# A hybrid encoder layer on one core: attention rotated by one head, three preparations moved

## The chip, the cores and the metric

The kernel runs on one core of one Trainium2 chip. The metric is the device time of one execution in microseconds (us); the median of three runs of the kernel before is 1181.16 us (1180.96 to 1181.49). A difference below 0.2%, about 2.4 us, is counted as no change.

## What is computed

One layer works on 512 prompt tokens and 64 sample tokens (576 columns here) of width 1024. The normed input `h` goes through one wide projection `w_in`, whose columns feed three branches, and the branches are merged by gates:

```python
glu_v, glu_g, conv_gate, z, xbc, dt_raw, q, xa_gate, gates = split(rmsnorm(x) @ w_in)
# A: causal depthwise conv of width 31, LayerNorm over channels
c = dwconv31(glu_v * sigmoid(glu_g))
out_a = (silu(layernorm(c)) * silu(conv_gate)) @ conv_out_w
# B: state-space scan (SSD) in chunks, 4 groups of 8 heads
out_b = (group_norm(ssd(silu(dwconv4(xbc)), dt) * silu(z))) @ ssd_out_w
# C: cross-attention, 4 heads of 256, 256 memory tokens
k, v = rmsnorm(mem) @ xa_kv_w          # the sample uses cached k, v
o = softmax(q k^T / 16) v
out_c = (o * silu(xa_gate)) @ xa_out_w
m = g0 * out_a + g1 * out_b + g2 * out_c
x_new = x + rmsnorm(m @ w_out)
```

Memory keys and values, convolution tails and SSD states are outputs too.

## The kernel before, in words

**Numbers.** Every large product is made in a reduced-width float type from a high and a low part of both operands: each weight `w` becomes `whi` (a copy rounded to that type) and `wlo = w - whi`, and so do the activations. One product is three matmuls: `whi` with the high activations, `whi` with the low, `wlo` with the high (`mac`, L206 to L216, and `proj`, L218). A projection of 128 columns over 576 tokens is 8 x 3 x 2 = 48 matmuls; in the attention a key block is 24 and the values of a head are 48.

**Weights.** The list `order` (L95 to L162) is a hand-written order of weight jobs. `W(name)` (L201) takes one and has `prep_to` prepare jobs up to two further on (LA = 2). Preparing is a load on the SP queue into one of three `raw` buffers, a copy to `whi` on ScalarE (L186), and the low part. Jobs ahead of `hold` (L144) take the low part on VectorE with one subtraction (L188). Jobs from `hold` on write minus `whi` by ScalarE (L190; here the copy of `raw` with scale -1) and add `raw` to it by an accumulating DMA on the POOL queue (L191). `whi` and `wlo` have three buffers each, so the job n+3 waits until the matmuls of job n have read theirs.

**Order of the work.** The program is written in straight line, and the tile framework orders each engine's instructions at build time by priority, which is the order of the program, and by when its own model of the chip thinks that operands and buffers are there. On the chip each engine then runs its list in order.

1. Input norm and transposes; then four SSD groups of five chunks (`chunk_a`, `chunk_b`), with projections (`fills`) as filling between the chunks.
2. Three `glu` tiles (L751; two projections each), in between the group norm of the last SSD group (`gating_b(3)`), then its output projection `out_b(3, 0..3)` (L755). Then the pools of this stage are closed.
3. The **pair phase** (L803 to L992): seventeen pairs of projections made with seven products each instead of eight (Strassen's scheme, products P1 to P7, 12 matmuls each, 119 slots in `seq`). It first builds four combinations of the activations, `T1` to `T4` (`comb`, L810 to L835), in a pool that opens here. `pair_load` fetches weights, `pair_pure` (L858) prepares a weight used alone with the accumulating DMA, `pair_sum` (L867) sums of weights on VectorE. The list `todo` (L973) says how many slots ahead each is issued. Results are attention gates `xg` and the gates `g2`, spilled to memory through the SP queue, the gates `g1`, and five more `glu` tiles.
4. **Attention** (L998 to L1174): memory tokens are loaded, normed (`rms_tile`) and transposed into `memT`; the queries of head 0 are projected ahead. Then, in a loop over four heads: keys and queries, keys to token order and cached keys transposed, values, scores and softmax in three tiles, transposes of the probabilities (L1152), their high and low parts (`pth`, `ptl`), output products, gating into `oc`.
5. `oc` is split into high and low parts, eight output projections `oc0..7` are merged; then LayerNorm sums over the convolution (`ln_mean`, `ln_rstd`), eight `cg` projections (the gate of branch A), eight `g0` projections, the LayerNorm applied tile by tile (L1253 on), eight `oa` projections, then `w_out` and the final norm.

**The convolution of width 31** is 240 instructions on VectorE (L773: 30 taps for each of 8 tiles). They lie in a list `bg`, from which `bgrun(n)` takes the next n and issues them with raised priority: one at every second slot of the pair phase, 44 per head, ten per merge, and all that are left before `ln_mean` (L1243). LayerNorm needs all of them.

**Names in the profile.** `mm<-hT,whi` is a projection of tokens, `ps<-memT,wlo` a key block, `ps<-wlo,memT` a values block; X, Y and Z (L892) are the PSUM tiles of the pair phase; `ct` its result tiles, `raw`/`rawb`, `ph`/`pl` its weights; `mt` the memory tokens; `P` the probabilities; `c` a convolution tile.

Of the kernel before, what the change touches and what calls it, by code (L numbers as in the profile page):

```python
# [8 lines left out]
F32 = mybir.dt.float32  # L9
# [19 lines left out]
def hybrid_trunk_kernel(  # L29
# [110 lines left out]
    for j in range(3):  # L140
        glu_jobs(j)
    for q in range(4):
        ob_job(3, q)
    hold = len(order)  # L144
    for h in range(4):
        if h == 0:
            for i in range(2):
                wjob(f"q{i}", w_in, C_Q + 128 * i)
        for i in (2 * h, 2 * h + 1):
            wjob(f"k{i}", xa_kv_w, 128 * i)  # L150
            if h > 0:
                wjob(f"q{i}", w_in, C_Q + 128 * i)
        for i in range(2):
            wjob(f"v{h}_{i}", xa_kv_w, 1024 + 256 * h, r0=512 * i, kk=4, cols=256)
# [14 lines left out]
    def prep_to(n):  # L169
        while nprep[0] <= min(n, len(order) - 1, limit[0]):  # L170
# [14 lines left out]
            else:  # L185
                a = nc.scalar.activation(hi[:, :n_], raw[:, :n_], AF.Copy)  # L186
                if nprep[0] < hold:
# [49 lines left out]
    hl = [st.enter_context(tc.tile_pool(name="hl4", bufs=4, reuse_waits="tile"))]  # L237

# [12 lines left out]
    for t in range(5):  # L251
# [3 lines left out]
        else:  # L255
            x_t = s2.tile([128, D], F32, tag="M", name="x4")
        nc.sync.dma_start(out=x_t[:n], in_=xp_d[128 * t:128 * t + 128] if t < 4 else xs_d)
        xt.append((x_t, n))
        if t == 0:
            wpre = s2.tile([128, D], F32, tag="R", name="wpre")  # L260
# [12 lines left out]
    sqx = s2.tile([128, D], F32, tag="M", name="sqx")  # L273
# [62 lines left out]
    eal = s2.tile([128, 32], F32, tag="yo", name="eal", bufs=1)  # L336
    nc.sync.dma_start(out=eal, in_=ssd_a_log[0].partition_broadcast(128))
    after = s2.tile([128, 128], F32, tag="bt", name="after")
# [8 lines left out]
    def dt_proj():  # L347
# [9 lines left out]
        dtv["raw"] = raw = s2.tile([64, 640], F32, tag="M", name="dtraw")  # L357
# [32 lines left out]
    def dt_cum():  # L390
# [13 lines left out]
        acsT = s2.tile([32, 640], F32, tag="M", name="acsT")  # L404
# [5 lines left out]
    vraw = s2.tile([104, 128], F32, tag="cbm", name="vraw")  # L410
# [9 lines left out]
    def load_t(dst, c0, src_ap, n, scale=1.0):  # L420
        raw = s2.tile([128, 128], F32, tag="bt", name="praw")
# [65 lines left out]
    def out_state(h, g, dst):  # L487
# [3 lines left out]
        o = s2.tile([128, 512], F32, tag="hio", name="ho", bufs=1)  # L491
# [8 lines left out]
    def chunk_a(g, c):  # L500
        nl = 128 if c < 4 else 64
        cs = slice(128 * c, 128 * c + nl)
        Rt = s2.tile([128, 8, 128], F32, tag="R", name="R")
# [3 lines left out]
        if c == 4:  # L507
            hin = s2.tile([128, 4, 128], F32, tag="hio", name="hin", bufs=1)
# [18 lines left out]
        cbm = s2.tile([128, 128], F32, tag="cbm", name="cbm")  # L527
        nc.vector.tensor_tensor(cbm[:nl, 0:nl], pc[:nl, 0:nl], mask[:nl, 0:nl], ALU.mult)
        bt = s2.tile([128, 128], F32, tag="bt", name="bt")
# [5 lines left out]
        xw = s2.tile([128, 512], F32, tag="xw", name="xw")  # L535
# [4 lines left out]
        xd = s2.tile([128, 512], F32, tag="xd", name="xd")  # L540
# [4 lines left out]
        cd = s2.tile([128, 8], F32, tag="cd", name="cd")  # L545
        nc.scalar.activation(cd, R[:, :, nl - 1], AF.Exp)
        Mt = s2.tile([128, 8, 128], F32, tag="M", name="M")
# [14 lines left out]
    def chunk_b(g, c, tup):  # L562
# [6 lines left out]
        if h is not None:  # L569
# [233 lines left out]
    def hb(i, j):  # L803
        ks, ts = slice(4 * i, 4 * i + 4), slice(288 * j, 288 * j + 288)
        return hT[0][:, ks, ts], hT[1][:, ks, ts]

# [3 lines left out]
    comb = {k: tuple(sp.tile([128, 4, 288], F32R, name=f"{k}{a}", bufs=1) for a in "hl") for k in ("T1", "T2", "T3", "T4")}  # L810
    for kp in range(2):
        ks = slice(2 * kp, 2 * kp + 2)

        def blk(i, j):
            f = th_tile().rearrange("p (k t) -> p k t", k=2)
            h, l = hb(i, j)
            nc.vector.tensor_tensor(f, h[:, ks].bitcast(F32), l[:, ks].bitcast(F32), ALU.add)
            return f

        def put(name, f):  # L820
            h, l = comb[name]
            nc.scalar.activation(h[:, ks], f, AF.Copy)
            nc.vector.tensor_tensor(l[:, ks], f, h[:, ks].bitcast(F32), ALU.subtract)

        a, b = blk(0, 1), blk(0, 0)
        nc.vector.tensor_tensor(b, b, a, ALU.subtract)
        put("T1", b)
        c = blk(1, 1)
        nc.vector.tensor_tensor(a, c, a, ALU.subtract)
        put("T3", a)  # L830
        nc.vector.scalar_tensor_tensor(c, b, -1.0, c, ALU.mult, ALU.subtract)
        put("T2", c)
        d = blk(1, 0)
        nc.vector.scalar_tensor_tensor(d, c, -1.0, d, ALU.mult, ALU.subtract)
        put("T4", d)  # L835
# [84 lines left out]
    def pair_use(kind, j, c):  # L920
# [11 lines left out]
        else:  # L932
            nc.sync.dma_start(out=spill["g2"][j], in_=c)
# [40 lines left out]
    for p in range(np_):  # L974
# [7 lines left out]
            (at[p, "P4"] - 6, lambda p=p: pair_pure(p, "W22", "P4")),  # L982
# [17 lines left out]
    st = ExitStack()  # L1000
    st3 = ExitStack()
    a2 = st3.enter_context(tc.tile_pool(name="a2", bufs=2, reuse_waits="tile"))
    memp = st3.enter_context(tc.tile_pool(name="memp", bufs=1, reuse_waits="tile"))
    st4 = ExitStack()
    m0 = st4.enter_context(tc.tile_pool(name="m0", bufs=1, reuse_waits="tile"))
    memT = [memp.tile([128, KD, NMEM], F32R, name=f"memT{i}") for i in range(2)]
    mt_ = []
# [398 lines left out]
```

## Time and profile before

| what | before |
|---|---|
| median of 3 runs | 1181.16 us |
| profiled execution, its own time | 1180.58 us |
| span of the profiled instructions | 1178.5 us |
| mean granted TensorE clock | 0.973 |
| TensorE matmul busy | 1113.5 us, 94% |
| VectorE busy | 854.8 us, 73% |
| ScalarE busy | 620.0 us, 53% |
| pair phase (first P2 to last product) | 501.4 to about 719 us |
| attention (first query projection to the first `oc` projection at full rate) | 719.2 to 914.5 us |

How to read it: "busy" is the share of the span in which an engine executes; the granted clock is the share of its full rate that TensorE was allowed. In a row of waits, `PE x Ln <- DMA y: a, b, c` says that instructions of TensorE at line n stood idle for a us in all, b times, at most c us, until a DMA into y had landed. In a row of windows stand the length, each engine's busy time with its number of instructions, the granted clock, the DMA engines' busy share and GB/s. In a group's row the first number behind the bar is the busy time in us, the second the mean of one instruction in ns.

### The profile page before, as it was taken

How to read it: one execution, taken by the hardware profiler on the slowest of the kernel's cores; microseconds unless marked ns; L12 is line 12 of the kernel's file. 1: busy time of each engine (PE TensorE's matmuls, PEld its weight loads, DVE VectorE, ACT ScalarE, POOL GpSimd, SP SyncE). 2: the span in 40 equal slices, each digit the busy share in tenths (PEclk: the TensorE clock that was granted, in tenths of full speed). 3: DMA queues.
4: the chain of work that ended last, by engine and by line, in shares of the span. 5: the costliest groups of instructions: out<-in, count | busy, mean ns of one | idle time of the engine just before them, and what ended most of it. 6: DMA issues, size and time to landing. Idle time of an engine off the chain costs nothing.

```text
span 1178.5 us, 20510 instructions
## 1 busy us (share of the span) xinstructions
PE 1113.5 (94%) x8081; PEld 1061.3 (90%) x8081; DVE 854.8 (73%) x1355; ACT 620.0 (53%) x1081; POOL 157.6 (13%) x253
## 2 busy tenths in 40 slices
PE   8999999999999999969999997788997999999997
PEld 8999999999999999959999997687886999999975
DVE  5878888597879766498888871477878988683433
ACT  5565655383456324266666664656446324684332
POOL 0100200020002001122233211101101111111000
PEclk9999999999999999979999999789988999999999
DMA  7354423432352322475888888669858886778822
GB/s 198 92 171 134 122 73 112 130 103 81 105 142 83 90 76 81 108 152 119 205 180 179 200 219 216 148 145 215 187 150 190 221 191 159 165 164 185 223 72 80
DMA packets 203797, 172.94 MB, mean 147 GB/s; under 512 B 15190, under 2 KB 175998, under 8 KB 203702
## 3 DMA queue, kind: packets, MB, share of 16 engines
q1 hardware_dynamic: 188294, 128.90, 37.6%
q0 software_dynamic: 15408, 42.74, 20.3%
q8 instruction: 63, 1.03, 0.4%
q14 instruction: 32, 0.26, 0.1%
HBM read 114.85 MB, written 14.03 MB: 109 GB/s over the span
## 4 chain that ended last, share of the span: by engine, by line
PE 78%; DMA 9%; issue 7%; ACT 2%; DVE 2%; POOL 0%; SPq 0%; DVEq 0%; POOLq 0%; ACTq 0%
PE mm L211 51%; PE X L892 7%; DMA wlo<-raw 4%; PE Y L892 4%; DMA pl<-rawb 2%; PE Z L892 2%; PE ps L211 2%; PE ps L1100 2%; PE ps L568 2%; PE ps L594 2%; PE ps L1101 1%; PE ps L1099 1%; PE ps L572 1%; DVE c L773 1%; DMA rawb<-in_w_in_dram 1%
## 5 line engine op out<-in xcount | busy, mean ns | idle before, releaser
L211 PE MATMUL mm<-hT,whi 128*128 128x288 f32 (+2 forms) x2240 | 401.4, 299 | 0.8 <-DVE hT L287 0.3
L211 PEld LDWEIGHTS mm<-hT,whi 128*128 128x128 f32 x2240 | 338.4, 191 | 3.5 <-issue 1.3
L211 PE MATMUL mm<-hT,wlo 128*128 128x288 f32 (+2 forms) x1120 | 249.3, 301 | 7.1 <-DMA wlo<-raw 7.1
L186 ACT ACTIVATE whi<-raw 128x1024 fp32r<-128x1024 f32 x118 | 124.8, 1058 | 246.0 <-PE mm L211 161.7
L773 DVE SCALAR_TENSOR_TENSOR c<-u,dww,c 128x606 f32<-128x606 f32 x240 | 202.2, 845 | 4.5 <-ACT c L766 0.8
L211 PEld LDWEIGHTS mm<-hT,wlo 128*128 128x128 f32 x1120 | 187.3, 191 | 10.1 <-DMA wlo<-raw 8.9
L211 PE MATMUL mm<-lo,whi 128*128 128x288 f32 x512 | 110.8, 296 | 1.7 <-DVE lo L613 1.7
L211 PE MATMUL mm<-hi,whi 128*128 128x288 f32 x512 | 110.8, 298 | 0.0
L211 PE MATMUL mm<-hi,wlo 128*128 128x288 f32 x512 | 110.2, 296 | 0.0
L188 DVE TENSOR_TENSOR wlo<-raw,whi 128x1024 fp32r<-128x1024 f32 x62 | 75.7, 1221 | 37.2 <-ACT whi L186 36.8
L191 POOL DMA_DIRECT2D wlo<-raw x56 | 48.7, 869 | 354.9 <-ACT wlo L190 238.3
L211 PEld LDWEIGHTS mm<-lo,whi 128*128 128x128 f32 x512 | 82.8, 188 | 1.9 <-DVE lo L613 1.9
L211 PEld LDWEIGHTS mm<-hi,whi 128*128 128x128 f32 x512 | 82.4, 188 | 0.9 <-issue 0.9
L211 PEld LDWEIGHTS mm<-hi,wlo 128*128 128x128 f32 x512 | 82.7, 188 | 0.2 <-issue 0.2
L190 ACT ACTIVATE wlo<-raw 128x1024 fp32r<-128x1024 f32 x56 | 58.7, 1049 | 14.0 <-PE ps L211 9.4
L461 DVE SCALAR_TENSOR_TENSOR acc<-xp,scw,acc 128x579 f32<-128x579 f32 x72 | 58.3, 814 | 3.1 <-ACT acc L457 1.9
L875 DVE TENSOR_TENSOR wlo<-sm,whi 128x1024 fp32r<-128x1024 f32 x34 | 41.5, 1220 | 10.1 <-ACT whi L874 10.0
L862 ACT ACTIVATE ph<-rawb 128x512 fp32r<-128x512 f32 x34 | 21.4, 630 | 50.1 <-PE X L892 36.8
L453 POOL COPY tails<-xp 128x3 f32<-128x3 f32 x24 | 18.9, 787 | 192.5 <-ACT xp L451 188.0
L874 ACT ACTIVATE whi<-sm 128x1024 fp32r<-128x1024 f32 x34 | 35.9, 1055 | 15.3 <-PE X L892 14.5
L864 POOL DMA_DIRECT2D pl<-rawb x34 | 30.2, 895 | 99.3 <-ACT pl L863 98.9
L665 DVE TENSOR_TENSOR ob<-ob,mm 128x576 f32<-128x576 f32 x24 | 18.0, 749 | 22.0 <-PE mm L211 21.9
(364 smaller groups left out, 2290.5 us busy)
## 6 DMA issues: line engine op xcount, KB each, us to landing
raw<-in_w_in_dram SPq DMA_DIRECT2D x70, 512.0 KB
wlo<-raw POOLq DMA_DIRECT2D x56, 512.0 KB, 5.6
raw<-in_w_in_dram SPq DMA_DIRECT2D x34, 256.0 KB
rawb<-in_w_in_dram SPq DMA_DIRECT2D x34, 256.0 KB
pl<-rawb POOLq DMA_DIRECT2D x34, 256.0 KB, 4.5
R<-scr SPq DMA_DIRECT2D x16, 512.0 KB
raw<-in_ssd_out_w_dram SPq DMA_DIRECT2D x16, 512.0 KB
raw<-in_xa_kv_w_dram SPq DMA_DIRECT2D x16, 512.0 KB
```

The costliest lines, as they stand in the source:

```text
L186: a = nc.scalar.activation(hi[:, :n_], raw[:, :n_], AF.Copy)
L188: b = nc.vector.tensor_tensor(lo[:, :n_], raw[:, :n_], hi[:, :n_].bitcast(F32), ALU.subtract)
L190: nc.scalar.activation(lo[:, :n_], raw[:, :n_], AF.Copy, scale=-1.0)
L191: nc.gpsimd.dma_start(out=lo[:, :n_], in_=raw[:, :n_], accum_op=ALU.add)
L211: m = nc.tensor.matmul(o, lhsT=w, rhs=r[:, s:s + w_], start=(i == 0 and a == 0), stop=(i == n - 1 and a == 2),)
L461: nc.vector.scalar_tensor_tensor(acc, xp[:, r:r + 579], w4[:, r, jt:jt + 1], acc, ALU.mult, ALU.add)
L568: nc.tensor.matmul(pS, lhsT=bt[:nl], rhs=xw[:nl], start=True, stop=True)
L773: nc.vector.scalar_tensor_tensor(c, upad[j][:, r:r + NC], w31[:, r, j:j + 1], c, ALU.mult, ALU.add)
L864: nc.gpsimd.dma_start(out=lo, in_=src, accum_op=ALU.add)
L874: nc.scalar.activation(hi, sm, AF.Copy)
L875: nc.vector.tensor_tensor(lo, sm, hi.bitcast(F32), ALU.subtract)
L892: nc.tensor.matmul(o, lhsT=w[:, k], rhs=r[:, k], start=(start and k == 0 and a == 0), stop=(k == 3 and a == 2), skip_group_check=True,)
```

## The change

- **Attention rotated by one head.** The body of the head loop is cut into five functions. One pass over h = 0 to 4 issues: keys and queries of head h; the transposes of the probabilities of head h-1; the key transposes of head h; the output products of head h-1; the values, scores and softmax of head h. In the fifth pass the projections `cg0` and `cg1` stand in place of keys and queries; they come out of the later `cg` loop, their results have a pool of their own (`keep`), and `ln_rstd` stands behind `cg4` instead of `cg2`, so again behind three projections. `bgrun` is called 41 times a head, and 12 times in the fifth pass, where it was 44 a head.
- **Activation combinations in the SSD chunk tiles' place.** The chunk tiles get a pool of their own (`sc`), closed after the last chunk; `T1` to `T4` are made in that space, ahead of `out_b(3, ..)`, with scratch tiles of the SSD stage. The third `glu` is made after `out_b(3, ..)` and after the closing of that stage's pool, straight ahead of the pair phase.
- **Memory tokens in the SSD output's place.** They are loaded and normed inside the pair phase, ahead of P5 of pair 8, in the space of `ob`, whose content has been spilled by then.
- **Low parts of keys by DVE.** Of the jobs behind `hold`, those whose names begin with k or v (eight keys, eight halves of values) take the low part by the subtraction on VectorE.
- Smaller: `pair_pure` is issued seven slots ahead instead of six; the spill of `g2` is issued on ScalarE's queue instead of SP's; cached values are loaded with the transposes of the probabilities.

The diff, cut to its core:

```diff
-    for j in range(3):
+    for j in range(2):
         glu_jobs(j)
     for q in range(4):
         ob_job(3, q)
+    glu_jobs(2)
     hold = len(order)
...
+    for j in range(2):
+        wjob(f"cg{j}", w_in, C_CG + 128 * j)
     for j in range(8):
         wjob(f"oc{j}", xa_out_w, 128 * j)
-    for j in range(8):
+    for j in range(2, 8):
         wjob(f"cg{j}", w_in, C_CG + 128 * j)
...
-                if nprep[0] < hold:
+                if nprep[0] < hold or name[0] in "kv":
                     b = nc.vector.tensor_tensor(lo[:, :n_], raw[:, :n_], hi[:, :n_].bitcast(F32), ALU.subtract)
...
-    for j in range(3):
-        glu(j, s2, "acc", 2)
-        if j == 0:
-            gating_b(3)
-    for q in range(4):
-        out_b(3, q)
-    st.close()
+    stc.close()
+    stt = ExitStack()
+    tcp = stt.enter_context(tc.tile_pool(name="tcp", bufs=1, side="right", reuse_waits="tile"))
+    glu(0, s2, "acc", 2)
+    gating_b(3)
+    glu(1, s2, "acc", 2)
...
-    comb = {k: tuple(sp.tile([128, 4, 288], F32R, name=f"{k}{a}", bufs=1) for a in "hl") for k in ("T1", "T2", "T3", "T4")}
+    comb = {k: tuple(tcp.tile([128, 4, 288], F32R, name=f"{k}{a}", bufs=1) for a in "hl") for k in ("T1", "T2", "T3", "T4")}
...
+    for q in range(4):
+        out_b(3, q)
+    st.close()
+    glu(2, sx, "bc", 4)
...
-            nc.sync.dma_start(out=spill["g2"][j], in_=c)
+            nc.scalar.dma_start(out=spill["g2"][j], in_=c)
...
-            (f - 6, lambda p=p: pair_pure(p, "W12", "P2")),
-            (at[p, "P1"] - 6, lambda p=p: pair_pure(p, "W11", "P1")),
+            (f - 7, lambda p=p: pair_pure(p, "W12", "P2")),
+            (at[p, "P1"] - 7, lambda p=p: pair_pure(p, "W11", "P1")),
...
+    mt_ = [(obf[:, D * t:D * t + D], 128) for t in range(2)]
+
+    def mem_prep():
+        for t, (m_t, _) in enumerate(mt_):
+            nc.sync.dma_start(out=m_t, in_=mem_prompt[0, 128 * t:128 * t + 128])
+            rms_tile(m_t, 128, obf[:, 2 * D:3 * D], ssx[:, t], None)
+
     for i, (p, pr) in enumerate(seq):
+        if (p, pr) == (8, "P5"):
+            mem_prep()
...
+    last, sgl = None, []
+    for h in range(5):
+        if h < 4:
+            khi, klo, ck, qhi, qlo, kfs = att_kq(h)
+        else:
+            for j in range(2):
+                sgl.append(silu2(proj(f"cg{j}"), keep, "sg", 2))
+                bgrun(6)
+        if last is not None:
+            b_ = att_pt(h - 1, last[1])
+        if h < 4:
+            ckh, ckl = att_k(h, ck, kfs)
+        if last is not None:
+            att_out(h - 1, last[0], *b_)
+        if h < 4:
+            last = att_scores(h, khi, klo, qhi, qlo, ckh, ckl)
...
-        sgs.append(silu2(proj(f"cg{j}"), hlA, "hi", 8))
-        if j == 2:
+        sgs.append(sgl[j] if j < 2 else silu2(proj(f"cg{j}"), hlA, "hi", 8))
+        if j == 4:
             ln_rstd()
```

More of the change, by code (lines that the diff above doesn't have):

```diff
@@ L356, in dt_proj @@
                     )
-        dtv["raw"] = raw = s2.tile([64, 640], F32, tag="M", name="dtraw")
+        dtv["raw"] = raw = sc.tile([64, 640], F32, tag="M", name="dtraw")
         nc.gpsimd.memset(raw[:, T:640], 0.0)
@@ L420, in load_t @@
     def load_t(dst, c0, src_ap, n, scale=1.0):
-        raw = s2.tile([128, 128], F32, tag="bt", name="praw")
+        raw = sc.tile([128, 128], F32, tag="bt", name="praw")
         nc.sync.dma_start(out=raw[:n], in_=src_ap)
@@ L539, in chunk_a @@
         )
-        xd = s2.tile([128, 512], F32, tag="xd", name="xd")
+        xd = sc.tile([128, 512], F32, tag="xd", name="xd")
         nc.vector.tensor_tensor(
@@ L749, in glu, with hb, blk, put @@
         u_tile(j, t, gate)
-    for j in range(3):
-        glu(j, s2, "acc", 2)
-        if j == 0:
-            gating_b(3)
+    stc.close()
[4 more added lines that the diff above has]
+    glu(1, s2, "acc", 2)
+    def hb(i, j):
+        ks, ts = slice(4 * i, 4 * i + 4), slice(288 * j, 288 * j + 288)
+        return hT[0][:, ks, ts], hT[1][:, ks, ts]
+    comb = {k: tuple(tcp.tile([128, 4, 288], F32R, name=f"{k}{a}", bufs=1) for a in "hl") for k in ("T1", "T2", "T3", "T4")}
+    for kp in range(2):
+        ks = slice(2 * kp, 2 * kp + 2)
+        def blk(i, j):
+            if j == 1:
+                f = s2.tile([128, 582], F32, tag="xp", name="xp")[:, 0:T].rearrange("p (k t) -> p k t", k=2)
+            else:
+                f = s2.tile([128, T], F32, tag="acc", name="f", bufs=2).rearrange("p (k t) -> p k t", k=2)
+            h, l = hb(i, j)
+            nc.vector.tensor_tensor(f, h[:, ks].bitcast(F32), l[:, ks].bitcast(F32), ALU.add)
+            return f
+        def put(name, f):
+            h, l = comb[name]
+            nc.scalar.activation(h[:, ks], f, AF.Copy)
+            nc.vector.tensor_tensor(l[:, ks], f, h[:, ks].bitcast(F32), ALU.subtract)
+        a, b = blk(0, 1), blk(0, 0)
+        nc.vector.tensor_tensor(b, b, a, ALU.subtract)
+        put("T1", b)
+        c = blk(1, 1)
+        nc.vector.tensor_tensor(a, c, a, ALU.subtract)
+        put("T3", a)
+        nc.vector.scalar_tensor_tensor(c, b, -1.0, c, ALU.mult, ALU.subtract)
+        put("T2", c)
+        d = blk(1, 0)
+        nc.vector.scalar_tensor_tensor(d, c, -1.0, d, ALU.mult, ALU.subtract)
+        put("T4", d)
     for q in range(4):
@@ L1000, in hybrid_trunk_kernel @@
     st = ExitStack()
+    keep = st.enter_context(tc.tile_pool(name="keep", bufs=2, reuse_waits="tile"))
     st3 = ExitStack()
@@ L1003, in hybrid_trunk_kernel @@
     memp = st3.enter_context(tc.tile_pool(name="memp", bufs=1, reuse_waits="tile"))
-    st4 = ExitStack()
-    m0 = st4.enter_context(tc.tile_pool(name="m0", bufs=1, reuse_waits="tile"))
+    stt.close()
     memT = [memp.tile([128, KD, NMEM], F32R, name=f"memT{i}") for i in range(2)]
-    mt_ = []
-    sqm = m0.tile([128, D], F32, name="sqm")
-    for t in range(2):
-        m_t = m0.tile([128, D], F32, tag="mt", name="mt", bufs=2)
-        nc.sync.dma_start(out=m_t, in_=mem_prompt[0, 128 * t:128 * t + 128])
-        mt_.append((m_t, 128))
-        rms_tile(m_t, 128, sqm, ssx[:, t], None)
     q0 = [proj(f"q{i}") for i in range(2)]
@@ L1101, in mac1, with att_kq @@
             nc.tensor.matmul(out, lhsT=wl, rhs=rh, start=False, stop=(i == n - 1))
-    for h in range(4):
+    def att_kq(h):
         khi = a1.tile([128, 2, 256], F32R, tag="khi", name="khi")
@@ L1118, in hybrid_trunk_kernel, with att_k @@
             bgrun(6)
+        return khi, klo, ck, qhi, qlo, kfs
+    def att_k(h, ck, kfs):
         token_major(kfs, o_mk, h)
@@ L1140, in hybrid_trunk_kernel, with att_pt @@
             Ps.append(softmax(ps, n, cnt))
+            bgrun(3)
+        return vhl, Ps
+    def att_pt(h, Ps):
+        cv = a1.tile([128, 2, 256], F32, tag="cv", name="cv")
+        nc.sync.dma_start(out=cv, in_=cache_mem_v[0, 0, :, h, :].rearrange("(m p) c -> p m c", p=128))
         sgs = []
@@ L1161, in hybrid_trunk_kernel, with att_out @@
         nc.scalar.activation(pts.rearrange("p m t -> p (m t)"), pp[:, :128], AF.Copy)
+        return cv, sgs, pth, ptl, pts
+    def att_out(h, vhl, cv, sgs, pth, ptl, pts):
+        vh, vl = vhl
         for i in range(2):
```

84 lines of the change are left out of this document (30 added, 54 removed).

## The prediction

> **What bounds the kernel now.** I read the page first, then the stages' windows, then TensorE's waits, then the chain of waits. The profiled execution took 1180.58 us, 2.1 more than its span; the median of the runs, 1181.16, is 0.6 above it. I add and subtract on 1180.58.
>
> ```profile
> span 1178.5 us, 20510 instructions
> core 0: us, PE busy (x) PEld busy (x) DVE busy (x) ACT busy (x) POOL busy (x), PEclk, DMA share, GB/s
> 437.00:501.40 64.40, 64.40 (x489) 63.24 (x489) 34.79 (x47) 21.65 (x31) 7.95 (x14) 1.00 0.32 90
> 501.40:540.00 38.60, 26.62 (x150) 23.43 (x149) 32.34 (x48) 22.24 (x39) 8.33 (x10) 0.82 0.62 126
> 540.00:719.20 179.20, 172.44 (x1284) 170.34 (x1284) 144.34 (x214) 117.34 (x205) 50.56 (x55) 1.00 0.80 189
> 719.20:787.50 68.30, 53.11 (x341) 48.33 (x341) 30.99 (x54) 36.76 (x67) 6.86 (x8) 0.85 0.75 182
> 787.50:831.00 43.50, 38.74 (x267) 36.28 (x267) 34.64 (x54) 23.14 (x42) 5.17 (x6) 0.92 0.76 183
> 831.00:875.50 44.50, 39.21 (x264) 37.13 (x263) 33.68 (x53) 23.13 (x42) 5.20 (x6) 0.88 0.75 179
> 875.50:914.50 39.00, 29.88 (x205) 26.95 (x204) 33.19 (x54) 26.30 (x49) 4.33 (x5) 0.87 0.78 180
> 1003.90:1068.90 65.00, 65.00 (x490) 65.00 (x489) 46.49 (x71) 48.64 (x64) 8.91 (x10) 1.00 0.74 166
> ```
>
> In the first and the last of these rows TensorE is busy throughout at full clock; nothing is to be had there. In the others it loses time in two ways: it stands idle (length less busy), and then runs at a lower granted clock (one less the clock, times the length). Both together, a little too much because the two overlap: 501.4 to 540 12.0 + 6.9 = 18.9 us; 540 to 719.2 6.8; then attention 15.2 + 10.2 = 25.4, 4.8 + 3.5 = 8.2, 5.3 + 5.3 = 10.6, 9.1 + 5.1 = 14.2. That is 84 us; the change aims at all of it. What ended TensorE's idle time:
>
> ```profile
> PE ps L211 <- DMA wlo<-raw: 8.0, 4, 3.5
> PE Z L892 <- DMA pl<-rawb: 7.4, 5, 2.8
> PE mm L211 <- DMA wlo<-raw: 7.1, 4, 3.0
> PE ps L326 <- DVE mt L269: 6.4, 2, 6.2
> PE ps L1152 <- ACT P L1093: 5.5, 1, 5.5
> PE ps L1099 <- ACT pth L1155: 3.0, 3, 1.0
> PE mm L211 <- DVE lo L613: 1.7, 1, 1.7
> ```
>
> Low parts by accumulating DMA lead the list: `ps` are values (and keys), `mm` queries. Then come the memory tokens, the last head's softmax, the high part of the probabilities.
>
> **Part by part: the start of the pair phase.** Durations:
>
> ```profile
> 485.64 4.02 DMA rawb<-in_w_in_dram
> L862 ACT ACTIVATE ph<-rawb 128x512 fp32r<-128x512 f32 x34 | 21.4, 630 | 50.1 <-PE X L892 36.8
> pl<-rawb POOLq DMA_DIRECT2D x34, 256.0 KB, 4.5
> L817 DVE TENSOR_TENSOR ct<-hT,hT 128x576 f32<-128x576 f32 x8 | 5.8, 749 | 0.0
> ```
>
> Making T1 to T4 is 24 VectorE instructions (8 sums of two parts, 8 combinations, 8 low parts), 24 x 0.749 = 18.0 us, now just where the products wait for them. Moved ahead of `out_b(3)`, they fall into the row 437 to 501.4, where VectorE is busy 34.8 of 64.4: 52.8 with them, so they are hidden; for an evacuation that queues behind them I put 1 us (0 to 5). What is late next is the first weights' low part: load 4.0, two ScalarE copies 1.3, POOL landing 4.5, together 9.8 us. Its cover is the third `glu`, 96 matmuls at 65.0/490 = 0.133 us, 12.8 us; without that cover the whole 9.8 would return. So I leave 4 of 18.9 (a clock window, the end of the first X chain) and 1 for the evacuations: 14 gained.
>
> **The rest of the pair phase.** Seven slots' lead instead of six gives 12 x 0.133 = 1.6 us more to low parts that are late by at most 2.8; of the 6.8 lost I count 3.9 as these waits and gain them. Against it stands `mem_prep` on ScalarE:
>
> ```profile
> 723.58 5.57 DMA spill_g<-ct
> 729.20 5.25 DMA mt<-in_mem_prompt_dram
> 734.47 1.15 ACT sqm L265 x2
> 735.64 1.28 ACT L266
> ...
> 812.68 7.62 PE mm L211 x44
> 820.30 0.67 PE ps L1152 x6
> ```
>
> Two squares at 1.15, two table loads at 1.28 (the square root, and back), two short roots: some 5.5 us on an engine busy 117.3 of 179.2. Behind it in the in-order queue stand the evacuations of X, Y and Z, for which TensorE waits beyond one slot of 1.6. Bounds 0 and 5.5; I take 1.5, near the lower end, since one instruction outlasts no slot. The spill of `g2` adds eight DMA issues to that queue, each behind a `tanh` of the same engine, so with no wait of its own: nothing. SP loses them: weight loads no longer queue behind a spill that waits for its tile. Net 2.4 gained. [...]
>
> **The transition.** The chain shows why the memory tokens are late: their tile lay where `ct` did and waited for the spill (5.57), then loaded (5.25). With the tokens ready before the phase ends, the 6.4 wait and the clock after it go; the values' first wait (3.5) goes with the low parts below. Of 25.4 I leave 6 (transposes of the tokens, a query's low part, one clock window): 19 gained.
>
> **The heads.** The chain's last two rows show queries of the next head (`mm`) already ahead of the probabilities' transposes: the framework has rotated part of it. What rotation adds is that keys and queries (2 x 24 and 2 x 48 matmuls) of head h+1 stand ahead of them in the program, and two projections after the last head. That covers the 5.5 of the last softmax and most of the 3.0. Low parts:
>
> ```profile
> L190 ACT ACTIVATE wlo<-raw 128x1024 fp32r<-128x1024 f32 x56 | 58.7, 1049 | 14.0 <-PE ps L211 9.4
> L188 DVE TENSOR_TENSOR wlo<-raw,whi 128x1024 fp32r<-128x1024 f32 x62 | 75.7, 1221 | 37.2 <-ACT whi L186 36.8
> wlo<-raw POOLq DMA_DIRECT2D x56, 512.0 KB, 5.6
> ```
>
> For 16 of the jobs, 1.05 us of ScalarE and 5.6 of landing are replaced by 1.22 us of VectorE: the 8.0 us of `ps` waits go. Queries keep the DMA; their 7.1 in four waits stays in part. Per head I leave 4 us: 1.0 for `pth`, 1.7 of clock, about 1 for a query. For the clock:
>
> ```profile
> 868.60:872.00 3.40, 3.40 (x10) 2.71 (x10) 3.33 (x6) 0.00 (x0) 0.00 (x0) 0.51 0.62 116
> 886.00:890.00 4.00, 2.25 (x18) 1.98 (x17) 3.25 (x5) 2.43 (x5) 0.88 (x1) 1.00 1.07 223
> 890.00:894.00 4.00, 4.00 (x35) 4.00 (x35) 2.97 (x4) 1.69 (x3) 0.00 (x0) 1.00 0.99 204
> ```
>
> A 3.4-us window at half clock follows the 1.0-us wait for `pth`, while 1.75 us idle at 888 bring none; so I let a remaining `pth` wait cost 1.7. [...] So 8.2, 10.6 and 14.2 shrink to 4 each: 21 gained, past 719.2 in all 40.
>
> **Whether VectorE allows it.** It gains 16 x 1.22 = 19.5 us and sheds 1.5 (two norms of the tokens).
>
> ```profile
> 719.20:914.50 195.30, 160.94 (x1072) 148.69 (x1071) 132.51 (x213) 109.32 (x200) 21.55 (x25) 0.88 0.76 181
> 719.20:1004.80 285.60, 251.24 (x1748) 238.99 (x1748) 214.42 (x318) 141.43 (x236) 32.78 (x38) 0.92 0.77 184
> 914.50:1004.80 90.30, 90.30 (x677) 90.30 (x678) 81.91 (x106) 32.12 (x37) 11.23 (x13) 1.00 0.80 191
> ...
> L773 DVE SCALAR_TENSOR_TENSOR c<-u,dww,c 128x606 f32<-128x606 f32 x240 | 202.2, 845 | 4.5 <-ACT c L766 0.8
> ```
> ```profile
> 1003.96 0.79 DVE L782 TENSOR_TENSOR csum<-csum,c 128x606 f32<-128x606 f32 x1
> 1065.49 1.43 DVE L615 SCALAR_TENSOR_TENSOR lo<-hi 128x576 fp32r<-128x576 f32 x2 [0.53 <-ACT hi L611]
> ```
> ```profile
> 1068.71 0.43 PE L211 MATMUL mm<-hi,whi 128*128 128x288 f32 x2
> ```
>
> The convolution ends at 1004.8, the LayerNorm chain behind it at 1066.9, and `oa0` begins at 1068.7. It needs the eighth tile after seven eighths of its 6.4 us, at 1074.3: 7.4 us of slack. So from 719.2 VectorE may take 285.6 + 7.4 = 293.0 us to the end of the convolution before a microsecond lost there is lost at the end; if TensorE gains 40, only 253. It has 214.4 + 18.0 = 232.4 us of work, so it must be busy 0.92 of the time. Where taps are at hand all the time (914.5 to 1004.8) it reaches 81.9/90.3 = 0.907. At 0.907 it takes 256.2: a gain of 36.8, not 40. I take 36.8. It is the tighter bound.
>
> **Sum:** 14 + 2.4 + 36.8 = 53.2; 1180.6 - 53.2 = 1127.4, say 1127. The convolution's instructions, `cg0`, `cg1` and all products stay the same in number.
>
> **Rivals.**
> - *Already rotated* (0.18). The rows of the chain speak for it. Then only the transition (19), the values' remaining waits (8.0 - 3.5 = 4.5), the first two gains (16.4) count: 1180.6 - 40 = 1141. Against it: the 5.5 wait of the last softmax has nothing to cover it now.
> - *VectorE in its order* (0.14). In attention it is busy 132.5/195.3 = 0.68, waiting in order for ScalarE and TensorE. If it comes to 0.80 from 719.2 on, the convolution takes 290.5 us, the gain there is 2.5, the time 1162. Against it: these waits are TensorE's own lateness passed on.
> - *Slower, by the same queue* (0.09). Taps, issued with raised priority, stand ahead of the new low parts, and TensorE waits for those at every key and value. At 0.70 the convolution takes 332 us, 39 more than allowed, against 16.4 gained: 1203. It decides from 232.4/(293.0 + 16.4) = 0.751, just what VectorE does over this stretch now (214.4/285.6). That is why this rival stays: with no better use of VectorE the change gains nothing.
> - *It meets there* (no change, 0.04): a use of 0.745 to 0.757, within 0.2% (2.4 us, what a measurement of this kernel can tell).
> [...]
>
> **How the numbers follow.** My forecast, about 1119 to 1136 (VectorE at 0.93 to 0.88), has 0.45; it is the likeliest, so the time is 1127. Faster by over 0.2%: 0.45 + 0.18 + 0.14 + 0.10 = 0.87; within 0.04; slower 0.09. The range leaves out the slower and unchanged cases (0.13) and the outer parts of the 0.14 and the 0.10: 1108 to 1163.
>
> **What would show it.** Right: between the third `glu` and the second pair TensorE shows under 5 us idle; no wait for `mt`; no `ps` wait for a DMA into `wlo`; a head takes 37 to 40 us instead of 44; VectorE over 0.87 busy from there to the convolution's end; then `oa0` waits a few us for the activations. Wrong: heads still of 43 us or more, `mm` or `ps` waiting for VectorE's `wlo`, VectorE under 0.8, new ScalarE waits around pair 8, or a queue of low parts at `out_b(3)`.

## The result and the profile after

The changed kernel takes 1141.95 us (median of 4 runs, 1140.47 to 1143.13) against 1181.1 beside it: ratio 0.9667, 95% interval 0.9651 to 0.9684. The forecast was 1127 with a range of 1108 to 1163: faster, as forecast, by 39 us instead of 54. The profiled execution took 1143.13 us.

The page and the stages' windows of the changed kernel (columns as in the prediction):

```profile
span 1141.4 us, 20485 instructions
PE 1097.9 (96%) x8081; PEld 1052.2 (92%) x8081; DVE 868.8 (76%) x1371; ACT 606.4 (53%) x1065; POOL 148.3 (13%) x237
```
```profile
437.00:517.40 80.40, 67.40 (x492) 65.43 (x491) 56.14 (x77) 33.01 (x49) 16.90 (x16) 0.92 0.37 92
517.40:540.00 22.60, 22.60 (x172) 22.60 (x171) 16.37 (x26) 14.80 (x26) 9.80 (x10) 1.00 0.75 162
540.00:720.20 180.20, 171.64 (x1259) 169.03 (x1258) 140.65 (x210) 118.67 (x208) 46.83 (x51) 0.99 0.80 189
720.20:890.20 170.00, 159.47 (x1168) 151.91 (x1166) 147.56 (x228) 95.52 (x183) 9.49 (x11) 0.96 0.65 167
720.20:976.10 255.90, 245.36 (x1812) 237.80 (x1811) 226.66 (x332) 126.91 (x219) 20.11 (x24) 0.97 0.69 174
```

Read against before, stage by stage. From 437 to the first product of the pair phase: 64.4 us before, 80.4 now, **16.0 lost**. The pair phase: 217.8 before (501.4 to 719.2), 202.8 now: 15.0 gained. Attention to the end of its heads: 195.3 before, 170.0 now, in which the two projections moved into it (12.8 us) are done as well: 38.1 gained. The rest is the same in both (251.2 + 12.8 = 264.0 before). 38.1 + 15.0 - 16.0 = 37.1 = 1178.5 - 1141.4. So the first stage, which in before stood at full clock without a gap, has become the place with the largest loss. TensorE's waits show it:

```profile
PE mm L214 <- DVE xs L657: 10.8, 1, 10.8
PE mm L214 <- DVE lo L618: 3.8, 2, 2.2
PE Y L905 <- ACT whi L887: 3.5, 2, 2.1
PE Z L905 <- DMA pl<-rawb: 3.3, 4, 1.3
PE ps L1139 <- ACT pts L1183: 2.9, 3, 1.2
PE ps L331 <- DVE memT L334: 2.3, 1, 2.3
```

The list that led the prediction (`wlo` by DMA, `mt`, the last `P`) is gone from it. The first row is new, and so are 2.2 us of the second (the other 1.6 are the wait for `lo` that stood in before with 1.7). The timeline of the changed kernel shows what they are (start, duration, engine):

```profile
462.98 0.43 PE L650 MATMUL ps<-tl,onesr 128*128 128x288 f32 x2
463.72 1.28 ACT L652 ACT_TABLE_LOAD   x1
465.01 0.89 ACT L652 ACTIVATE rs<-ps,eps 128x288 f32<-128x288 f32 x2
467.02 3.75 DVE L653 RECIPROCAL rs<-rs 128x576 f32<-128x576 f32 x1
470.69 0.70 DVE L778 TENSOR_TENSOR f<-hT,hT 128x576 f32<-128x576 f32 x1
471.30 0.75 DVE L778 TENSOR_TENSOR xp<-hT,hT 128x576 f32<-128x576 f32 x1
471.96 0.75 DVE L784 TENSOR_TENSOR T4l<-f,T4h 128x576 fp32r<-128x576 f32 x1
472.63 3.00 DVE L657 SCALAR_TENSOR_TENSOR xs<-xs,vecs,rs 128x576 f32<-128x576 f32 x4
474.21 1.33 PE L214 MATMUL mm<-hi,whi 128*128 128x288 f32 x4 [10.81 <-DVE xs L657]
```

This is the last group norm, `gating_b(3)`: its sum on TensorE, a table load and two roots on ScalarE, a reciprocal of 3.75 us on VectorE, scalings, splits; `out_b(3)` needs all of it. Before, the same chain ran at nearly the same time:

```profile
466.86 3.75 DVE L648 RECIPROCAL rs<-rs 128x576 f32<-128x576 f32 x1 [1.99 <-ACT rs L647]
470.65 3.01 DVE L652 SCALAR_TENSOR_TENSOR xs<-xs,vecs,rs 128x576 f32<-128x576 f32 x4
```

There the third `glu` (12.8 us of products) lay over it: TensorE made its products without a gap until `out_b(3)` began at 475.94. The change put that `glu` behind `out_b(3)`, and the chain lay bare. Besides, three instructions of the combinations stand between reciprocal and scalings (470.69 to 472.63). The clock pays too: half speed from 467.1 to 480.8, in which TensorE works 4.4 us for 2.2 us' worth.

### The profile page after: what moved, and what is told of

Same layout as the page of the kernel before. It is cut to its first block, busy times and chain, and to the rows that moved or that the text cites. A ratio compares the mean times of both kernels' runs of the same rounds, so it can differ in the third digit from the quotient of the medians.

```text
span 1141.4 us, 20485 instructions
## 1 busy us (share of the span) xinstructions
PE 1097.9 (96%) x8081; PEld 1052.2 (92%) x8081; DVE 868.8 (76%) x1371; ACT 606.4 (53%) x1065; POOL 148.3 (13%) x237
## 4 chain that ended last, share of the span: by engine, by line
PE 84%; DVE 7%; issue 3%; DMA 3%; ACT 2%; POOL 0%; DVEq 0%; SPq 0%; ACTq 0%; POOLq 0%
PE mm L214 55%; PE X L905 7%; DVE c L816 3%; PE Y L905 3%; PE ps L214 3%; PE Z L905 2%; PE ps L1114 2%; PE ps L1115 2%; PE ps L1113 2%; DMA pl<-rawb 2%; PE ps L573 2%; PE ps L599 2%; PE ps L577 1%; DVE wlo L191 1%; PE ps L538 1%
## 5 line engine op out<-in xcount | busy, mean ns | idle before, releaser
L214 PE MATMUL mm<-hT,whi 128*128 128x288 f32 (+2 forms) x2240 | 397.3, 297 | 1.0 <-ACT ob L668 0.5
L214 PEld LDWEIGHTS mm<-hT,whi 128*128 128x128 f32 x2240 | 334.3, 189 | 3.4 <-issue 1.3
L214 PE MATMUL mm<-hT,wlo 128*128 128x288 f32 (+2 forms) x1120 | 246.4, 298 | 0.0
L816 DVE SCALAR_TENSOR_TENSOR c<-u,dww,c 128x606 f32<-128x606 f32 x240 | 199.6, 846 | 2.8 <-ACT c L809 0.3
L214 PEld LDWEIGHTS mm<-hT,wlo 128*128 128x128 f32 x1120 | 184.8, 189 | 1.3 <-issue 0.7
L191 DVE TENSOR_TENSOR wlo<-raw,whi 128x1024 fp32r<-128x1024 f32 x78 | 95.2, 1221 | 51.2 <-ACT whi L189 50.8
L214 PE MATMUL mm<-hi,whi 128*128 128x288 f32 x512 | 112.3, 301 | 10.8 <-DVE xs L657 10.8
L194 POOL DMA_DIRECT2D wlo<-raw x40 | 34.7, 868 | 329.9 <-ACT wlo L193 257.4
L193 ACT ACTIVATE wlo<-raw 128x1024 fp32r<-128x1024 f32 x40 | 42.0, 1049 | 27.8 <-PE ps L214 27.8
L559 ACT ACTIVATE M<-R,tok 128x128 f32<-128x128 f32 (+1 forms) x80 | 24.8, 380 | 12.3 <-PE ps L599 12.3
```

Of the source, the lines that this page charges most:

```text
L191: b = nc.vector.tensor_tensor(lo[:, :n_], raw[:, :n_], hi[:, :n_].bitcast(F32), ALU.subtract)
L193: nc.scalar.activation(lo[:, :n_], raw[:, :n_], AF.Copy, scale=-1.0)
L194: nc.gpsimd.dma_start(out=lo[:, :n_], in_=raw[:, :n_], accum_op=ALU.add)
L214: m = nc.tensor.matmul(o, lhsT=w, rhs=r[:, s:s + w_], start=(i == 0 and a == 0), stop=(i == n - 1 and a == 2),)
L559: nc.scalar.activation(M[:, 4 + e, :], R[:nl, 4 + e, :], AF.Relu, scale=-1.0, bias=tok[:nl, 0, c, a + 4:a + 5])
L816: nc.vector.scalar_tensor_tensor(c, upad[j][:, r:r + NC], w31[:, r, j:j + 1], c, ALU.mult, ALU.add)
```

## The experiments

Each ran in three rounds beside the kernel before, whose medians on the chips used were 1177.7 to 1179.25 us. Ratios are to that kernel; to set one beside the change, take its ratio less 0.9667, times 1180 us.

**The hole: cover or queue.** Theory cover: the moved `glu` no longer lies over the norm's chain. Rival queue: the 18 us of combinations on VectorE hold the norm up.

*Third glu ahead of `out_b(3)` again*, the rest as changed:

```
+    glu(2, s2, "acc", 2)
     for q in range(4):
         out_b(3, q)
     st.close()
-    glu(2, sx, "bc", 4)
```


> Against the changed kernel's 1142. Theory (cover): the 10.8 us that TensorE now stands idle ahead of out_b(3), with the half clock behind it, come because the third glu no longer covers the chain of the last group norm (table load, root, reciprocal, scaling, splits: 11.5 us). With the third glu back ahead of out_b(3) that hole closes (-16 us), and a smaller one opens at the first pair, whose low part has no cover now (ScalarE copy, POOL issue, landing 4.5, a clock window: 7 to 10 us): 1135 (1131 to 1139). Rival (queue): the combinations' 18 us of VectorE instructions, queued among the group norm's, make it late wherever the glu stands: still some 10 us idle ahead of out_b(3), and the hole at the first pair besides: 1148 to 1152.

Measured 1142.64 us, ratio 0.9681 (0.9658 to 0.9704): neither figure. A wait of 10.4 us is still there, but another one (timeline of this kernel):

```profile
484.35 1.28 ACT L745 ACT_TABLE_LOAD   x1
485.64 0.60 ACT L745 ACTIVATE acc<-mm 128x512 f32<-128x512 f32 x1
486.41 0.85 PE L213 MATMUL mm<-hi,whi 128*128 128x288 f32 x2 [10.39 <-ACT acc L746]
```

The norm's chain is covered now (`xs` was scaled from 474.8 on, with products until 476). But the `glu`'s `tanh` needs a tile `acc`, of which there are two. By the program the combinations use both, and VectorE works on them until about 484; with the `tanh` waits the PSUM tile that `out_b(3)` wants. A wait for the chain was exchanged for a wait for a scratch tile; in the kernels below that avoid this conflict, it is gone.

*Combinations behind `out_b(3)` in the program*, the rest as changed:

```
+    for q in range(4):
+        out_b(3, q)
     comb = {k: tuple(tcp.tile([128, 4, 288], F32R, name=f"{k}{a}", bufs=1) for a in "hl") for k in ("T1", "T2", "T3", "T4")}
...
-    for q in range(4):
-        out_b(3, q)
     st.close()
```


> The changed kernel with T1 to T4 made behind out_b(3) in the program, the third glu left where the change put it. Theory (cover): only the 2 us by which combinations stand ahead of the scaling and the 2.2 us ahead of the first low part go, and part of the clock window: 1138 (1135 to 1140), with 7 us or more still idle ahead of out_b(3). Rival (queue): the hole closes nearly whole, 1126 to 1130.

Measured 1143.17 us, 0.9688 (0.9669 to 0.9706), with the hole as it was (10.81 and 2.15 us). This told nothing of the queue: the framework orders each engine's work by when it can start, and its instruction queues came out in the order of the changed kernel, on all engines. It is a second sample of the change, and says how far two samples of one program lie apart: 0.2%.

*Both covers*: third `glu` ahead of `out_b(3)`, the fourth behind it, combinations behind it in the program, the memory tokens one pair earlier:

```
+    glu(2, s2, "acc", 2)
+    for q in range(4):
+        out_b(3, q)
     comb = {k: tuple(tcp.tile([128, 4, 288], F32R, name=f"{k}{a}", bufs=1) for a in "hl") for k in ("T1", "T2", "T3", "T4")}
...
-    glu(2, sx, "bc", 4)
+    glu(3, sx, "bc", 4)
...
-        if (p, pr) == (8, "P5"):
+        if (p, pr) == (7, "P5"):
```


> Third glu ahead of out_b(3), a fourth glu (taken out of the pairs, made as two plain projections) behind it, combinations behind out_b(3). Both theories: no hole of more than 2 us at either place, for 96 matmuls instead of 84, 1.6 us more: 1128 (1124 to 1132). If VectorE, with one convolution tile's input earlier and the combinations later, becomes late in the pair phase: 1134 or more.

Measured 1130.61 us, 0.9582 (0.9562 to 0.9603), as expected. Of the hole there is left:

```profile
PE mm L214 <- DVE u L752: 0.7, 1, 0.7
PE mm L214 <- DVE lo L618: 0.3, 1, 0.3
```

*Norm first*: the `glu` stays where the change put it; the first sum of each half of the combinations takes the tile of the norm's root, so that VectorE can make it only behind the scalings:

```
-            if j == 1:
-                f = s2.tile([128, 582], F32, tag="xp", name="xp")[:, 0:T].rearrange("p (k t) -> p k t", k=2)
+            if (i, j) == (0, 1):
+                f = s2.tile([128, T], F32, tag="tot", name="f", bufs=1).rearrange("p (k t) -> p k t", k=2)
             else:
-                f = s2.tile([128, T], F32, tag="acc", name="f", bufs=2).rearrange("p (k t) -> p k t", k=2)
+                f = s2.tile([128, 582], F32, tag="xp", name="xp")[:, 0:T].rearrange("p (k t) -> p k t", k=2)
```


> Of the changed kernel only the scratch tiles of the combinations differ: the first sum of each half lies in the tile of the group norm's root, so that VectorE makes it behind the four scalings of the last group norm, and the other sums lie in the tiles of the convolution's inputs. The queue of VectorE then has reciprocal, scalings and the first low parts of the last group norm with nothing of the combinations between them. The third glu stays behind out_b(3). In the changed kernel TensorE stands 10.81 us and then 2.15 us ahead of and in out_b(3), and the clock is at half for 13.7 us. Theory cover (the third glu no longer lies over the group norm's chain): VectorE's share of the hole goes, 2.0 us before the scalings and about 2 before the low parts, and 8.5 us or more remain, with the clock after it: 1138 us (1136 to 1141). Rival queue (the combinations on VectorE make the hole): the hole is 3 us or less: 1128 us (1126 to 1131).

Measured 1139.8 us, 0.9656 (0.9625 to 0.9687). The waits of the hole:

```profile
PE mm L214 <- DVE xs L657: 7.9, 1, 7.9
PE mm L214 <- DVE ob L670: 1.1, 1, 1.1
PE mm L214 <- DVE lo L618: 0.8, 1, 0.8
```

The first and the last stand in place of 10.8 and 2.2: 8.7 us instead of 13.0, so the queue's share was 4.3 us and the bare chain's is 8.7. The wait for `ob` is new: an evacuation of `out_b(3)` now stands behind the combinations, so 3.2 us are saved in all. Both theories held a part; cover the larger. In time these 3 us can't be told from nothing.

*Third glu ahead and norm first together*, the `glu` with a tile of the four `bc`:

```
+    glu(2, sx, "bc", 4)
     for q in range(4):
         out_b(3, q)
```


> Of the changed kernel: the third glu stands ahead of out_b(3) again, with its tile among the tanh tiles of four buffers, and the combinations take scratch tiles that are free only behind the scalings of the last group norm, so that neither the glu's tile nor the norm waits for them. The pair phase then begins straight behind out_b(3). Theory cover: TensorE has work during the group norm's chain, the hole of 10.8 + 2.2 us ahead of out_b(3) is under 1.5 us, and the clock stays full; where the pair phase begins, the first low parts of its weights may be late by some us, less than the 9.8 that their making takes, since the hole that let them be made is gone: 1132 us (1128 to 1137). Rival (one cover cannot serve both): the 9.8 us come back in full at the start of the pair phase, with clock: 1141 us (1138 to 1146).

Measured 1133.32 us, 0.9613 (0.9582 to 0.9644). Windows from 437 to the pair phase and on to 540:

```profile
437.00:502.30 65.30, 64.59 (x490) 63.20 (x489) 49.57 (x70) 26.52 (x39) 9.05 (x14) 1.00 0.26 75
502.30:540.00 37.70, 34.71 (x234) 33.77 (x235) 27.96 (x41) 24.69 (x43) 13.16 (x14) 0.91 0.90 193
```

The hole is gone, at full clock, with VectorE at 49.57 of 65.30: all combinations fit there. What comes back at the start of the pair phase is 3.0 us of idle time and 6.8 us of half clock, not the 9.8 us that making the first weights takes. So without any cover at the pair phase's start the kernel is still 0.5% faster than the changed one (which lacks the better order on VectorE too): the cover was worth more where it had been.

*The start as before*: glus, `out_b(3)` and combinations in before's order and place, everything else changed:

```
     glu(0, s2, "acc", 2)
     gating_b(3)
     glu(1, s2, "acc", 2)
...
+    glu(2, s2, "acc", 2)
+    for q in range(4):
+        out_b(3, q)
+    st.close()
...
-    comb = {k: tuple(tcp.tile([128, 4, 288], F32R, name=f"{k}{a}", bufs=1) for a in "hl") for k in ("T1", "T2", "T3", "T4")}
+    comb = {k: tuple(sp.tile([128, 4, 288], F32R, name=f"{k}{a}", bufs=1) for a in "hl") for k in ("T1", "T2", "T3", "T4")}
```


> The changed kernel with three glus, out_b(3) and then the combinations in the pair phase's own pool, as before the change; all else changed. Theory: what the pair phase gained (15 us) was lost ahead of out_b(3) (16 us), so this part of the change is worth nothing: 1141 (1137 to 1145). Rival: the new place of the combinations helps the later stages too (other addresses, VectorE freed early): 1150 or more.

Measured 1145.33 us, 0.9723 (0.9692 to 0.9753), 0.3 us above the theory's range. Its windows show the loss of before again, at its old place:

```profile
437.00:502.10 65.10, 65.10 (x495) 63.94 (x494) 35.38 (x48) 25.36 (x39) 11.62 (x18) 1.00 0.42 108
502.10:540.00 37.90, 25.80 (x132) 23.33 (x131) 30.15 (x44) 17.07 (x29) 4.33 (x5) 0.73 0.43 90
```

The whole new start of the pair phase is worth 2 us by the medians of this chip (against 1143.17, the kernel with the combinations behind `out_b(3)`, whose queues are those of the change) and 7 by the ratios.

**Attention: which part pays.** *Low parts of keys and values by the accumulating DMA again*:

```
-                if nprep[0] < hold or name[0] in "kv":
+                if nprep[0] < hold:
```


> Of the changed kernel only the low parts of the key and value weights go back to the accumulating DMA (with a copy on ScalarE); rotation, tokens and the start of the pair phase stay as changed. Theory of the prediction (a low part by DMA is late, 8.0 us of waits in before, and each wait takes clock with it): 1152 us (1148 to 1158), with waits of ps for a DMA into wlo. Rival cover (with rotation the weights are ready early enough, so that the way of making them does not matter): 1142 us (1140 to 1145). Rival VectorE (its 19.5 us of low parts are what holds attention now): faster, 1135 us (1130 to 1139).

Measured 1154.04 us, 0.9783 (0.9753 to 0.9812): 14 us slower than the change, as the prediction's theory has it. Waits and window of its attention:

```profile
PE ps L1139 <- ACT pts L1183: 3.6, 2, 1.8
PE ps L214 <- DMA wlo<-raw: 3.3, 1, 3.3
PE ps L331 <- DVE memT L334: 2.7, 1, 2.7
```
```profile
718.40:893.50 175.10, 161.14 (x1157) 154.03 (x1157) 134.33 (x214) 106.83 (x195) 23.34 (x27) 0.94 0.88 205
```

Only one wait of `ps` for the DMA is left where before had four, so the rest of the change, rotation most likely, hides the others. But the stage is 8.3 us longer than the changed kernel's 166.8 (720.2 to 887.0, the same work), which is nearly all of the 8.7 between the spans of the two profiled executions (this one was among the kernel's faster). Besides the 3.3, ScalarE makes 16 copies more and TensorE waits longer for it (`pts` up to 1.8 instead of 1.2), and the clock is 0.94 instead of 0.96.

*Heads in the old order*, the two projections behind the last head:

```
-        if last is not None:
-            b_ = att_pt(h - 1, last[1])
...
+        khi, klo, ck, qhi, qlo, kfs = att_kq(h)
+        ckh, ckl = att_k(h, ck, kfs)
+        vhl, Ps = att_scores(h, khi, klo, qhi, qlo, ckh, ckl)
+        b_ = att_pt(h, Ps)
+        att_out(h, vhl, *b_)
```


> Of the changed kernel only the order of the heads goes back: keys and queries, scores, transposes and output of one head behind each other, and the two projections behind the last head. Low parts by VectorE, tokens and the start stay as changed. Theory of the prediction (rotation covers the softmax of the last head, 5.5 us, and the waits for the high part of the probabilities, 3.0, each with its clock): 1155 us (1151 to 1160). Rival already rotated (the framework had moved the next head's queries ahead by itself): 1143 us (1141 to 1147), what remains being the last head's softmax.

Measured 1150.73 us, 0.9756 (0.9725 to 0.9787): 10 us slower than the change, just under the theory's range and clear of the rival's. The waits of its attention name what rotation covers:

```profile
PE mm L214 <- DMA wlo<-raw: 4.4, 4, 1.9
PE ps L1174 <- ACT P L1107: 4.1, 3, 2.5
PE ps L1181 <- ACT P L1107: 1.1, 1, 1.1
```

The rival "already rotated" falls, although its time, 1141, is the one measured.

**The memory tokens.** *Loaded and normed at the start of attention again*, in tiles of a pool of its own in the place of the pair phase's:

```
-        if (p, pr) == (8, "P5"):
-            mem_prep()
...
+        nc.sync.dma_start(out=m_t, in_=mem_prompt[0, 128 * t:128 * t + 128])
+        rms_tile(m_t, 128, sqm, ssx[:, t], None)
```


> Of the changed kernel only the memory tokens go back: loaded and normed at the start of attention, into tiles in the place of the pair phase's spill tiles, instead of beside pair 8. Theory of the prediction (the tiles wait for the last spill, 5.6 us, and then for the load, 5.3; TensorE waits and loses clock): 1154 us (1150 to 1158), with a wait for mt of 5 to 7 us. Rival (the load alone is late, and other work of attention now lies over part of it): 1145 us (1142 to 1148).

Measured 1140.44 us, 0.9664 (0.964 to 0.9688): no slower at all; both theories miss. Waits in its pair phase, and at its tokens:

```profile
PE Z L905 <- DMA pl<-rawb: 2.2, 2, 1.6
```
```profile
PE ps L331 <- DVE mt L274: 3.0, 2, 2.8
```

The wait for `mt` is 3.0 us, where before had 6.4, and a stretch of half clock follows it (a transpose of the tokens takes 421 ns there, against 273 in the changed kernel, medians of 16). But the pair phase takes 195.9 us instead of 202.8 (200.9 to 202.8 in the five profiles in which that phase is as in the changed kernel): the waits for `whi`, 3.5 us in the changed kernel, and the clock after them (0.51 for 3.5 us from 596.8) do not come; from 540 to 714.7 the clock is 1.00 here. One pays for the other.

*The same with the spills on SyncE's queue again*:

```
-            nc.scalar.dma_start(out=spill["g2"][j], in_=c)
+            nc.sync.dma_start(out=spill["g2"][j], in_=c)
```


> As the kernel with the memory tokens loaded late again, and besides the spills of the last gate go back to SyncE's queue; rotation, low parts by VectorE and the start stay as changed. Theory spill (what made the tokens late in before was the spill, queued behind weight loads on SyncE, and the change cured it by moving the spill): the wait for mt is 5 to 7 us again, 1147 us (1144 to 1151). Rival (the spill's queue does not matter; the end of the phase came earlier for other reasons): the wait stays at 2.8 us, 1140 us (1138 to 1142).

Measured 1139.17 us, 0.9674 (0.9633 to 0.9716): the theory of the spill's queue falls too. SyncE's queue in it:

```profile
718.56 0.50 SPq L946 DMA_DIRECT2D spill_g<-ct  x1
719.15 0.91 SPq L1026 DMA_DIRECT2D mt<-in_mem_prompt_dram  x2
```

The load goes out 0.6 us behind the last spill's issue; in before it went out 5.6 us behind it, when the spill had landed (723.58, 729.20 in the prediction's chain). So the tokens no longer wait for a spill to land. By the code that is because the combinations have left that pool and moved its layout; no run tried that alone.

*Tokens loaded beside pair 8, but normed at the start of attention*:

```
-            rms_tile(m_t, 128, obf[:, 2 * D:3 * D], ssx[:, t], None)
...
+    for t, (m_t, _) in enumerate(mt_):
+        rms_tile(m_t, 128, sqm, ssx[:, t], None)
```


> Of the changed kernel only the norm of the memory tokens moves: their load stays beside pair 8, their squares, roots and scalings come at the start of attention, beside the first query's products (13 us). Theory ScalarE (the norm's instructions on ScalarE, with two table loads, delay the combined weights' high parts beside pair 8, so that the pair phase is 6 us longer than with the tokens loaded late): the pair phase takes 196 to 198 us instead of 202.8, the tokens are normed before the queries are done, and no new wait comes: 1136 us (1133 to 1138). Rival (the norm is late at its new place, as costly as where it was): 1141 us (1139 to 1143).

Measured 1141.64 us (1134.38 to 1143.03), 0.967 (0.9627 to 0.9714): the theory of ScalarE falls. The waits for `whi` are gone, but the pair phase still takes 200.8 us; other waits have taken their place. Its waits, and from its chain the longest piece near the loads:

```profile
PE Z L905 <- DMA pl<-rawb: 5.5, 4, 2.3
```
```profile
557.44 7.37 DMA pl<-rawb
```

The waits for `pl` by DMA and for `whi` together make 4.6 to 6.8 us in the five profiles with load and norm beside pair 8, 5.5 here with the load alone, and 2.2 and 2.3 in the two with neither. Between 548 and 575 us the low parts by DMA land after at most 5.2 us without the tokens' loads, and in each of the six profiles with them one takes 7.2 to 7.7, such as the one above. So the 1 MB of loads is the likelier cost, not the norm's instructions. It is not shown: the kernel before, which loads no tokens there, has low parts that land after 7.2 and 6.1 us (551.9, 561.06), though its pairs lie otherwise, and loads alone against nothing, in one kernel, was not tried.

**The sum of the good parts**: both covers, norm first, tokens normed late.

> The sum of what the runs so far gave: the third glu ahead of out_b(3) and the fourth behind it, the combinations behind the last group norm's scalings on VectorE, and the memory tokens loaded beside pair 7 but normed at the start of attention; rotation, low parts by VectorE and the spill on ScalarE's queue as in the changed kernel. If the parts add up: the kernel with both covers, 1130.6, less 4 to 6 for the norm, and 0 to 1 for the order on VectorE: 1126 us (1123 to 1129). Rival (the parts overlap, since the wait beside pair 8 only moves into the next): 1130 us (1129 to 1133).

Measured 1131.19 us, 0.959 (0.9556 to 0.9623): as fast as both covers alone, 0.8% faster than the change. The rival held: the parts do not add up. Against the profile of both covers (its slowest run, 1134.81) the stretch from 437 got 3.0 us shorter, the pair phase 7.8 (186.2 against 194.0), but attention 4.1 and the part behind it 3.2 longer. Waits of TensorE behind attention, of which the changed kernel has only the one for `ysq`:

```profile
PE mm L214 <- DVE lo L620: 1.5, 1, 1.5
PE mm L214 <- DMA wlo<-raw: 1.2, 1, 1.2
PE ps L1405 <- ACT ysq L1402: 0.8, 1, 0.8
PE mm L214 <- ACT hi L616: 0.5, 1, 0.5
```

The split tiles that `oa0` takes from ScalarE and VectorE (`hi`, `lo`) come too late here. In the changed kernel the last `lo` ends at 1036.25 and `oa0`, begun at 1031.64, comes to its tile at 1037.25: 1.0 us of room. Here VectorE's bound begins to bite.

## Why the prediction was partly right

**Past 719.2, the largest term: right.** Forecast 36.8 us gained, measured 38.1. VectorE was to take 256.2 us at a use of 0.907; it took 255.9 at 226.66/255.9 = 0.886. That the two agree so well is luck: 5.7 us less work than the 232.4 reckoned made up for the lower use. And the bound that the 36.8 was taken from did not bind: `oa0` waited for nothing, with 1.0 us of room, so VectorE was close to it but TensorE set the time, and its own 40 was 1.9 too high. Low parts (14 us) and rotation (10) are shown separately, by one kernel each; these 24 us are not all of the 38.1, and no run took both back, so how far each hides the other's waits stays open. The heads follow each other in 36 to 38 us instead of 42 to 46.

**The start of the pair phase: the step that failed.** The prediction counted 14 us here and 2.4 in the rest of the pair phase, with the third `glu` as cover for the first weights. The pair phase did gain 15.0 us. But the same `glu` had been the cover of the last group norm, a chain of 11.5 us, and moving it uncovered that: 16.0 us lost, which the prediction had put at nothing. I had read the row 437 to 501.4 (TensorE busy throughout, full clock) as "nothing is to be had there", and did not ask what kept it full. From 437 to the end of the pair phase both kernels take the same (282.2 and 283.2 us), where 16.4 were to be gained: 17.4 us missed, 1.3 won in attention, which is the whole difference to 1127. Two of its signs of being wrong came true: low parts waited for at `out_b(3)` (2.2 us), and waits for ScalarE around pair 8 (`whi`, 3.5 us).

**The combinations: mis-sized.** They do fit beside other work, as said. But "for an evacuation that queues behind them I put 1 us": in the changed kernel they cost the norm 4.3 us, within the bounds of 0 to 5. The second resource, the two `acc` tiles, I had not looked at; it costs 10.4 us as soon as a `glu` needs one of them.

**`mem_prep`: too cheap.** I put 1.5 us for its instructions on ScalarE and nothing for its two loads of 512 KB. With loads and norm the phase is 5 to 7 us longer than without either, and with the loads alone it is still 4.9 us longer (200.8 against 195.9). That the loads do it by delaying the pairs' own low parts is likely, not shown. The lead of seven slots was not tried by itself.

**The transition: right in size, half of the remedy needless.** The wait of 6.4 went, as forecast. But half of it goes with the tokens loaded late as well, once their load need not wait for a spill, which the prediction had read rightly as the first cause. The other half is saved by loading them early, and that costs in the pair phase what it saves.

**The clock: right, its price too simple.** Short waits do cost clock here: in before a step at half clock follows the wait of 1.00 us for `pth` at 867.4. No run shows an attention in which they cost none, the case of the 0.10 among the chances: of the changed kernel's, with waits of at most 2.3 us, 13.7 us are still at half clock. But 1.7 us for each wait of 1.0 us was too much: in the steps counted in the last section it is the idle time of a whole step, from 1.1 us on, that half clock follows.

## What to carry to other kernels

When a piece of work is moved to hide something, list first what it hides where it stands: a stage without a gap is full because something fills it, and its price is that of the chain below. Give scratch tiles and queues the same question as cover: who else needs this tile, and what stands behind this instruction on its engine. And try the parts of a change one by one: here two parts of attention paid some 24 us, the tokens nothing, and the start, put right, paid 6 to 10 more than as it was made.

## What the runs showed of the hardware

In the traces of before and of the changed kernel the clock changes on a grid. All starts of half-clock stretches between 440 and 1100 us, 9 and 5, lie in each of the two within 0.02 us on one grid of 3.41 us, and the stretches last one to four steps of it. In the changed kernel they start at 467.13, 596.84, 736.79, 815.29 and 880.15 us: 38, 41, 23 and 19 steps apart. Ahead of each of the 14 stands a step with 1.14 us or more of idle time of TensorE, in one wait or several. Two pairs of steps of the changed kernel:

```profile
774.30:777.80 3.50, 2.63 (x19) 1.78 (x17) 2.99 (x5) 3.24 (x7) 0.00 (x0) 1.00 0.08 9
777.80:781.20 3.40, 2.81 (x14) 2.41 (x15) 3.37 (x6) 0.27 (x1) 0.00 (x0) 1.00 0.95 299
811.90:815.30 3.40, 1.83 (x9) 1.32 (x10) 3.40 (x6) 1.54 (x4) 0.00 (x0) 1.00 0.47 101
815.30:818.70 3.40, 3.40 (x12) 2.82 (x11) 3.40 (x7) 0.00 (x0) 0.00 (x0) 0.50 0.64 212
```

Similar waits, 0.84 and 0.62 us at 776, 0.83 and 1.06 at 812, fall in two steps the first time (0.87 and 0.59 us idle) and in one step the second (1.57): only the second costs a step at half clock. Counted over the steps at full clock from 440 to 1000 us of both traces: of 19 with 0.5 to 1.1 us idle none is followed by half clock, of 15 with 1.1 to 1.75 us 5 are, of 9 with 2.0 us or more all are; what tells the 5 from the others is open. The two rows on the clock in the prediction fit this: the step ahead of its 868.60 held 1.15 us of idle time, while the 1.75 us near 888 fell into two steps, 0.99 and 0.76. So here some 1.5 us of waits were free or cost another 1.7 us by where they fell, which may be part of why samples of one program lie 0.2% apart.
